# Hybrid SSD and GLA trunk on one core: z of two groups, and the values of a head pair, projected together with weights 512 columns wide

## The chip, the core and the metric

One core of a Trainium2 chip runs the whole layer in one launch. The time is device time in microseconds (us): the median of several executions. Beside it stands one execution that the hardware profiler recorded; its rows are what the text reads. TensorE (PE) multiplies, with its weight loads (PEld) beside it; VectorE (DVE), ScalarE (ACT) and GpSimd (POOL) do the rest; SyncE (SP) mainly starts transfers. L12 is line 12 of the kernel file.

## The reference, cut to what matters

The model width is 1024, the sequence 2048 tokens behind 16 meta tokens, one layer. One projection of the normalized input `u` gives everything; two branches run as recurrences (16 SSD heads in 4 groups; 4 GLA heads of 128 keys and 256 values); gates merge them.

```python
proj = jnp.einsum('bld,dn->bln', u, w_in)
z, xbc, dt_raw, q, k, v, g_gla, a_lr, merge_g = split_cols(proj, IN_WIDTHS)
xbc = jax.nn.silu(causal_depthwise_conv(xbc, conv_w, conv_b))
...
y_m, s_m = ssd_chunked(xs[:, :m], dt[:, :m], a, bm[:, :m], cm[:, :m], N_META, s0)
y_r, _ = ssd_chunked(xs[:, m:], dt[:, m:], a, bm[:, m:], cm[:, m:], SSD_CHUNK, s_m)
y = jnp.concatenate([y_m, y_r], axis=1) + d_skip[:, None] * xs
y = y.reshape(b, l, D_SSD) * jax.nn.silu(z)
y_ssd = rmsnorm(y.reshape(b, l, SSD_GROUPS, D_SSD // SSD_GROUPS),
                ssd_norm_w.reshape(SSD_GROUPS, -1)).reshape(b, l, D_SSD)
...
o_r, _ = gla_chunked(q[:, m:], k[:, m:], v[:, m:], log_a[:, m:], GLA_CHUNK, st_m)
o = rmsnorm(jnp.concatenate([o_m, o_r], axis=1), gla_norm_w)
y_gla = o.reshape(b, l, GLA_DV) * jax.nn.silu(g_gla)
branches = jnp.stack([y_ssd.astype(y_gla.dtype), y_gla], axis=2)
branch_proj = jnp.einsum('blnc,ncd->blnd', branches, w_branch)
gates = jax.nn.sigmoid(merge_g.reshape(b, l, N_BRANCH, D_MODEL))
merged = jnp.sum(gates * branch_proj, axis=2)
return hres + jnp.einsum('bld,de->ble', merged, w_out)
```

Each SSD group needs 256 columns of z, each GLA head 256 columns of v. Both are used with tokens on the partitions.

## The kernel before, in words

The kernel has two parts. The first goes through the sequence in four blocks of 512 tokens, computes the projections and both recurrences, and writes their outputs to DRAM. The second computes the gates, the branch products and the output product; the change leaves it as it is, but for two buffers that it reads at its start (below). Block 0 also carries the 16 meta tokens, so its feature-major projections run in two segments of 264 columns.

*Products.* An fp32 operand is split into two parts, high and low, each of TensorE's rounded fp32 type. `accum` makes one product out of three matmuls (high by high, high by low, low by high; L193 to L195 before, L203 to L205 after). K is 1024, in eight slices (`kt`) of 128.

*Weights.* `load_w` fetches 512 columns of weights into `whl` (four buffers, high and low). The first time, in block 0, it takes them raw, ScalarE and GpSimd split them, and the split pair is stored to DRAM; later blocks fetch that pair.

*Two kinds of projection.* Feature-major (`proj_feat`): the weights are TensorE's stationary operand and `u` streams, 512 columns at a time (`pj<-u,whl`). Token-major (`proj_tok`): 128 tokens of `u` are stationary and weights stream (`pj<-whl,u`). Before, z of one group and values of one head are 256 columns wide: four chunks of tokens, eight slices, three matmuls, 256 columns each, 96 matmuls. Two chunks share one PSUM bank (`halves_of`), so such a projection takes two banks. In block 0 the values of the meta tokens are one more chunk: the high and low meta rows side by side (`both`), two matmuls a slice (L227 before, L239 after), into a bank of `pt`. Group 0's z is projected with other columns, 288 wide, in a projection of its own (`zm`), into three banks of `pj` and one of `pt`.

*PSUM.* Eight banks: `pj` has three buffers (projections), `pt` three (transposes, sums), `pc` two (products of the scans).

*Order.* The program is written with generators. A projecting generator (`ssd_proj`, then `gla_proj`) yields after every step; a step of projection is 24 matmuls of 512 columns or, before, 48 of 256, about 5.5 us. At each yield `step()` advances every running scan (`ssd_scan`, `gla_scan`) and side job (`gates`, `fetch_u` for the next block's `u`, `beside_unit`) by one of its own yields. So a few scan instructions stand behind each projection step. TensorE's and SyncE's instructions stand in exactly this written order; those of VectorE, ScalarE and GpSimd are placed by the scheduler of the language, fixed at build time.

*One block.* Group 0 to 3: z (two steps; it yields once in the middle), then four feature tiles (x twice, B, C), each with a causal convolution (eviction at L528 and L529 on ScalarE, three VectorE steps, tanh and product). Then the group's scan begins (`begin(ssd_scan(...))`): per chunk of 128 tokens `before(c)` makes three transposes into a `pt` bank (L595 before, L626 after) and VectorE reads them three times (L598, L600, L601; after L629, L631, L632); `after(c)` makes `py` in a `pc` bank (L619 and L620; after L650, L651), `pst` in another (L623; after L654), and VectorE reads `py` twice (L628 and L631; after L659 and L662). At its end stand two turns (transposes, L655, after L686) into `pt` banks, which ScalarE reads (L657). Then head 0 to 3: query, key (`gla_keys`), values (two steps), two gates (`gla_gates`), and the head's scan. It starts with `kd` (L747), in block 0 copies the meta rows' `kd` (L803, after L866) and transposes them (L805, after L868); it builds the meta state (L819, after L882) and its copy (L820), levels of a masked product in `pc` banks (`level_out`, L789, after L852; merged by a predicated copy, L796), and ends with turns and their product (L916).

*Buffers in SBUF.* z, values and scan outputs use `tok4` (five buffers of 128x1024 fp32). `end_ot` and `end_g0`, `end_g1` hold the last head's output and gates until the second part.

Of the kernel before, what the change touches and what calls it, by code (L numbers as in the profile page):

```python
# [14 lines left out]
P = 128  # L15
# [5 lines left out]
SG = 4  # L21
# [19 lines left out]
def trunk_kernel(ctx: ExitStack, tc: tile.TileContext, xm, xmt, w_feat, w_tok, w_zm, w_br, w_o,  # L41
# [17 lines left out]
    end_ot = base.tile([P, NCH, 256], F32, name="end_ot")  # L59
    end_gs = [base.tile([P, BLK], F32, name=f"end_g{j}") for j in range(2)]  # L60
# [124 lines left out]

    def save(n):

        while len(unsaved) > n:
            nc.sync.dma_start(*unsaved.pop(0))
# [19 lines left out]
    def proj_tok(key, src, u, starts, banks, width=256, per=2, sub=None, both=None):  # L209

        nq = KT // per
        opened = set()
        for q0 in range(0, nq, 2):
            if q0 == nq // 2:
                yield
            ws = [load_w(f"{key}_{q}", src[:, q * per * width:(q + 1) * per * width]) for q in (q0, q0 + 1)]
            for i, ((bk, ps), a) in enumerate(zip(banks, starts)):
                c0 = sub if sub is not None and i >= NCH else 0  # L220
                for k2 in range(2 * per):
                    kt = q0 * per + k2
                    h, lo = ws[k2 // per]
                    cs = slice(k2 % per * width + c0, (k2 % per + 1) * width)
                    if both is not None and i >= NCH:
                        for part in (h, lo):
                            nc.tensor.matmul(ps[:2 * META], both[:, kt], part[:, cs], start=kt == 0 and part is h,  # L227
                                             stop=kt == KT - 1 and part is lo)
                        continue
                    accum(ps[:, c0:width], tuple(t[:, kt, a:a + P] for t in u),  # L230
                          (h[:, cs], lo[:, cs]), bk not in opened, kt == KT - 1, skip_group_check=True)
                    opened.add(bk)
# [271 lines left out]
    def ssd_proj(o, g):  # L504
        m0, tt = o.m0, o.tt
        feats = []
        zs = mk(wk, [P, NCH, 256], F32, "tok4", bufs=NT4)
        if g == 0:
            pss = [bank(*pl) for pl in [(pj, "pj")] * 3 + [(pt, "pt")] + ([(pc, "pc")] if m0 else [])]
            yield from proj_tok("zm", w_zm, o.u, o.starts + [0] * o.ci0, list(enumerate(pss)), 288, 1, 256)  # L510
            begin(dt_chain(o, pss[NCH:] + pss[:NCH]))
            done = [(ps[:, :256], zs[:, c]) for c, ps in enumerate(pss[:NCH])]
        else:
            pss, places = halves_of(pj, "pj")
            yield from proj_tok(f"z{g}", w_tok[g], o.u, o.starts, places)
            done = [(ps, zs[:, 2 * r:2 * r + 2].rearrange("p c f -> p (c f)")) for r, ps in enumerate(pss)]
        for ps, dst in done:
            nc.scalar.activation(dst, ps, AF.Tanh, scale=0.5)
            nc.vector.scalar_tensor_tensor(dst, dst, 1.0, ps, op0=ALU.add, op1=ALU.mult)
        yield  # L520
# [19 lines left out]
        begin(ssd_scan(o, g, feats, zs))  # L540
# [7 lines left out]
    def ssd_scan(o, g, feats, zs):  # L548
# [64 lines left out]
        def after(c):  # L613
# [19 lines left out]
            nc.vector.tensor_tensor(yt[:, c], yof, zs[:, c], op=ALU.mult)  # L633
# [37 lines left out]

    def gla_values(o, h):
# [9 lines left out]
        yield from proj_tok(f"v{h}", w_tok[SG + h], o.u, o.starts + [0] * o.ci0, places, both=o.both)  # L682
# [6 lines left out]
    def gla_gates(o, h, gs):  # L689
        t0 = T_GLA + 4 * h  # L690
        end = o.b == nblk - 1 and h == GH - 1
        for j in range(2):
# [6 lines left out]
            gg = end_gs[j] if end else mk(wk, [P, BLK], F32, "gg", bufs=4)  # L699
# [5 lines left out]
    def gla_proj(o, h):  # L705
        got = {"gs": []}
        keys = yield from gla_keys(o, h)
        last = o.b == nblk - 1
        if last and h == GH - 1:
            begin(gla_scan(o, h, *keys, got))  # L710
            yield
            got["v"] = yield from gla_values(o, h)
            yield
            yield from gla_gates(o, h - 1, held_gates.pop())
            yield from gla_gates(o, h, got["gs"])
        else:
            yield
            got["v"] = yield from gla_values(o, h)
            if last and h == GH - 2:
                begin(gla_scan(o, h, *keys, got))  # L720
                held_gates.append(got["gs"])
                yield
            else:
                yield
                yield from gla_gates(o, h, got["gs"])
                begin(gla_scan(o, h, *keys, got))

    held_gates = []

    def gla_scan(o, h, qs, kf, got):  # L730
# [145 lines left out]
        ot = end_ot if very_last else mk(wk, [P, NCH, 256], F32, "ot", bufs=1)  # L876
# [44 lines left out]
    def begin(gen):  # L921
        begun.append(gen)
# [13 lines left out]
    with tc.manual_schedule(engines={mybir.EngineType.PE, mybir.EngineType.SP}):  # L936
        for b in range(nblk):
            o = new_block(b, next_u[b])
            for i in range(SG + GH):
                if (b, i) in beside:  # L940
                    begin(beside_unit(beside[b, i]))
                if i == 1:
                    begin(gates(o))
# [251 lines left out]
    with tc.manual_schedule(engines={mybir.EngineType.PE, mybir.EngineType.SP}):  # L1195
        run(-1)
        for i, (st, n, p) in enumerate(order):
            step_no[0] = i
            st.product(n, p)
            if i == 1:  # L1200
                gla_turn(end_ot, end_gs, pb, "psb")
# [7 lines left out]
def _layout(inputs):  # L1209
# [26 lines left out]
    w_tok = tiles(np.concatenate([cols(o_z, 1024), cols(o_v, 1024)], axis=1), 256)  # L1236
# [34 lines left out]
    return {"xm": xm, "xmt": xmt, "w_feat": w_feat, "w_tok": w_tok, "w_zm": w_zm, "w_br": w_br, "w_o": w_o, "cf32": cf32, "cmsk": cmsk.reshape(P, -1),  # L1271
# [21 lines left out]
```

## Time and profile before

| what | value |
|---|---|
| time, median of 3 executions | 2274.29 us (2273.98 to 2274.93) |
| profiled execution: its time, its span | 2277.34 us, 2275.6 us |
| mean granted TensorE clock | 0.996 |
| TensorE busy | 2216.7 us, 12599 matmuls |
| VectorE, ScalarE, GpSimd busy | 1626.3, 1119.0, 511.8 us |
| moved by DMA | 507.50 MB, mean 223 GB/s |

The span runs from the first to the last recorded instruction; the time of an execution takes in what lies around it. Busy time is a sum over instructions; for TensorE the matmuls are pipelined and the recorded ends are modelled, so the time of a row of matmuls is best read as the distance between two places in the timeline. A wait is given as `engine buffer line <- engine that released it, its buffer and line: total us, how many, longest`. A row of the timeline is start, length, engine, line and operation, `out<-in`, the two tile shapes in partitions and columns, the number of them, and in brackets a wait ahead of it with its releaser. A row of a stretch is its bounds, its length, then busy time and count, the granted clock, the DMA share and GB/s.

### The profile page before, as it was taken

What the parts mean: (1) busy time and instruction counts of PE and PEld (TensorE: products, weight loads), DVE (VectorE), ACT (ScalarE), POOL (GpSimd) and SP (SyncE); (2) the same over time, 40 slices, a digit from 0 to 9 for tenths busy, and PEclk for the clock granted to TensorE, in tenths of its full rate; (3) what the DMA queues carried; (4) which work ended last, traced back from release to release, by engine and by line L of the source; (5) the groups of instructions that cost most, each with busy time, mean ns of one, the idle gap of its engine ahead of it and who ended that gap; (6) DMA issues with size and microseconds to landing.
All of it is one profiled execution on the core that took longest, in us unless ns stands there. A gap on an engine that the chain in (4) does not pass through costs nothing.

```text
span 2275.6 us, 36414 instructions
## 1 busy us (share of the span) xinstructions
PE 2216.7 (97%) x12599; PEld 1936.4 (85%) x12599; DVE 1626.3 (71%) x3332; ACT 1119.0 (49%) x2508; POOL 511.8 (22%) x645
## 2 busy tenths in 40 slices
PE   6899999999999999999999999989999999999997
PEld 6899888889888988888988898868888888888886
DVE  5787766687775578676569755786778866787866
ACT  5565654454444444443455443464644545554443
POOL 3344533122321222221122100012111112111212
PEclk9999999999999999999999999999999999999999
DMA  7666865667886676887577655465769866878753
GB/s 255 223 227 228 300 231 208 208 196 239 266 281 204 196 221 216 267 269 228 185 225 225 220 189 166 154 228 193 255 216 293 242 203 201 283 269 232 206 164 111
DMA packets 281865, 507.50 MB, mean 223 GB/s; under 512 B 27104, under 2 KB 134880, under 8 KB 281680
## 3 DMA queue, kind: packets, MB, share of 16 engines
q1 hardware_dynamic: 217232, 413.76, 55.9%
q0 software_dynamic: 17568, 50.87, 7.2%
q10 hardware_dynamic: 46880, 40.54, 5.4%
q8 instruction: 99, 1.62, 0.3%
q14 instruction: 86, 0.70, 0.1%
HBM read 357.87 MB, written 147.19 MB: 222 GB/s over the span
## 4 chain that ended last, share of the span: by engine, by line
PE 79%; DVE 8%; DMA 5%; issue 3%; ACT 3%; POOL 1%; SPq 1%; ACTq 0%; POOLq 0%; DVEq 0%
PE pj L193 13%; PE pj L195 12%; PE pj L194 12%; PE psa L193 6%; PE psa L194 6%; PE psa L195 6%; PE psb L194 3%; PE psb L193 3%; PE psb L195 3%; PE pc L619 2%; PE pc L789 2%; PE psc L194 1%; PE psc L193 1%; PE psc L195 1%; PE pc L620 1%
## 5 line engine op out<-in xcount | busy, mean ns | idle before, releaser
L193 PE MATMUL pj<-u,whl 128*128 128x512 f32 (+1 forms) x1184 | 445.8, 377 | 10.0 <-ACT acc L529 5.0
L195 PE MATMUL pj<-u,whl 128*128 128x512 f32 (+1 forms) x1184 | 430.1, 363 | 0.0
L194 PE MATMUL pj<-u,whl 128*128 128x512 f32 (+1 forms) x1184 | 429.3, 363 | 0.0
L193 PE MATMUL pj<-whl,u 128*128 128x256 f32 (+1 forms) x992 | 288.6, 291 | 2.3 <-ACT u L261 2.2
L195 PE MATMUL pj<-whl,u 128*128 128x256 f32 (+1 forms) x992 | 282.2, 284 | 0.2 <-DVE u L266 0.2
L194 PE MATMUL pj<-whl,u 128*128 128x256 f32 (+1 forms) x992 | 282.0, 284 | 0.0
L193 PEld LDWEIGHTS pj<-u,whl 128*128 128x128 f32 x1184 | 224.1, 189 | 47.7 <-ACT acc L529 6.1
L195 PEld LDWEIGHTS pj<-u,whl 128*128 128x128 f32 x1184 | 223.7, 189 | 35.6
L193 PE MATMUL psa<-b,a 128*128 128x512 f32 x640 | 249.8, 390 | 4.1 <-ACT sn L1063 4.1
L194 PEld LDWEIGHTS pj<-u,whl 128*128 128x128 f32 x1184 | 224.3, 189 | 33.0
L195 PE MATMUL psa<-b,a 128*128 128x512 f32 x640 | 249.3, 390 | 0.7 <-DVE a L1047 0.7
L194 PE MATMUL psa<-b,a 128*128 128x512 f32 x640 | 249.1, 389 | 0.0
L193 PEld LDWEIGHTS pj<-whl,u 128*128 128x128 f32 x992 | 189.7, 191 | 4.1 <-ACT u L261 2.3
L195 PEld LDWEIGHTS pj<-whl,u 128*128 128x128 f32 x992 | 189.5, 191 | 0.8 <-DVE u L266 0.8
L194 PEld LDWEIGHTS pj<-whl,u 128*128 128x128 f32 x992 | 189.8, 191 | 0.4
L181 POOL TENSOR_TENSOR whl<-wr,whl 128x512 fp32r<-128x512 f32 (+1 forms) x100 | 138.8, 1395 | 187.1 <-ACT whl L180 150.9
L533 DVE SCALAR_TENSOR_TENSOR acc<-cin,hcw,acc 128x512 f32<-128x512 f32 (+1 forms) x192 | 160.4, 835 | 13.1 <-ACT acc L529 10.9
L1047 DVE TENSOR_TENSOR a<-ar,a 128x512 fp32r<-128x512 f32 x160 | 109.9, 690 | 82.0 <-ACT a L1046 81.3
L84 POOL TENSOR_TENSOR wr<-wr 128x256 f32<-128x256 f32 x80 | 72.3, 904 | 423.0 <-DMA wr<-u 159.9
L1022 ACT ACTIVATE b<-br 128x512 fp32r<-128x512 f32 x196 | 118.3, 626 | 58.2 <-DMA br<-br_t 19.8
L193 PEld LDWEIGHTS psa<-b,a 128*128 128x128 f32 x640 | 120.2, 188 | 31.2 <-ACT sn L1063 6.2
L195 PEld LDWEIGHTS psa<-b,a 128*128 128x128 f32 x640 | 120.2, 188 | 26.4 <-DVE a L1047 1.4
(297 smaller groups left out, 4839.1 us busy)
## 6 DMA issues: line engine op xcount, KB each, us to landing
whl<-k_s SPq DMA_DIRECT2D x96, 512.0 KB, 4.5
whl<-k_g SPq DMA_DIRECT2D x96, 512.0 KB, 4.2
whl<-k_v SPq DMA_DIRECT2D x48, 512.0 KB, 4.0
whl<-k_z SPq DMA_DIRECT2D x36, 512.0 KB, 3.9
wr<-in_w_feat SPq DMA_DIRECT2D x64, 256.0 KB, 4.4
k_s<-whl SPq DMA_DIRECT2D x32, 512.0 KB, 3.8
cb<-cumd ACTq DMA_DIRECT2D x64, 256.0 KB, 5.7
k_g<-whl SPq DMA_DIRECT2D x32, 512.0 KB, 3.9
```

The source lines that it names most:

```text
L84: (nc.vector if store is None else nc.gpsimd).tensor_tensor(o, x, y, op=ALU.subtract)
L181: nc.gpsimd.tensor_tensor(hl[:, 1], raw, hl[:, 0].bitcast(F32), op=ALU.subtract)
L193: nc.tensor.matmul(ps, sh, mh, start=first, stop=False, **kw)
L194: nc.tensor.matmul(ps, sh, ml, start=False, stop=False, **kw)
L195: nc.tensor.matmul(ps, sl, mh, start=False, stop=last, **kw)
L533: nc.vector.scalar_tensor_tensor(acc, cin[:, k:k + tt], hcw[:, ti, k:k + 1], acc, op0=ALU.mult, op1=ALU.add)
L619: nc.tensor.matmul(py[:, h * 64:(h + 1) * 64], dm[:, h], xdt[:, h], start=True, stop=True)
L620: nc.tensor.matmul(py[:, 256:512], cf[:, a:a + P], s_ssd[:, g], start=True, stop=True)
L789: nc.tensor.matmul(ps[:, r * P:(r + 1) * P], kq[:, 2 * r * P:(2 * r + 1) * P], kq[:, (2 * r + 1) * P:(2 * r + 2) * P], start=True, stop=True)
L1022: nc.scalar.activation(t[:, 0], raw, AF.Copy)
L1047: nc.vector.tensor_tensor(t[:, 1], src, t[:, 0].bitcast(F32), op=ALU.subtract)
```

## The change

- Group 1's z and group 2's z are projected together (`z12`), with weights 512 columns wide, after group 1's feature tiles. Each of the four token chunks fills a whole bank: the three of `pj` and one of `pt` (`four_banks`). The projection takes four steps of 24 matmuls. Group 1's scan begins at its second yield, and z of group 1 is looked up when the scan multiplies by it; group 2 has no projection of z. Group 0 and group 3 project z as before.
- The values of heads 0 and 1, and of 2 and 3, are projected together (`gla_pair`), in the even head, 512 columns wide, in four steps and four banks. The odd head's values wait in SBUF: for head 1 in two tiles (`shared`) that hold the last head's output and gates later, for head 3 in `tok4`. In the even head the scan begins ahead of its gates; the odd head has keys, gates, scan.
- In block 0 the pair's meta rows, 512 columns, accumulate in a `pc` bank.
- In the last block heads 2 and 3 keep projections of 256 columns; their weights are the halves of the stored wide arrays, so each `whl` takes two transfers (`load_half`).
- Evictions of a wide bank (tanh and product for z, split in two parts for values) are made per 256 columns. The block's `gates` begin at group 3 instead of group 1.

```diff
+    def load_half(key, q, head):
+        hl = mk(wpool, [P, 2, 512], F32R, "whl", bufs=4)
+        for k in range(2):
+            nc.sync.dma_start(hl[:, :, k * 256:(k + 1) * 256].bitcast(F32),
+                              kept[f"{key}_{2 * q + k}"][:, :, head * 256:(head + 1) * 256])
+        return hl[:, 0], hl[:, 1]
...
-    def proj_tok(key, src, u, starts, banks, width=256, per=2, sub=None, both=None):
+    def proj_tok(key, src, u, starts, banks, width=256, per=2, sub=None, both=None, head=None):
         nq = KT // per
+        every = 2 if width == 512 else nq // 2
         for q0 in range(0, nq, 2):
-            if q0 == nq // 2:
+            if q0 and q0 % every == 0:
                 yield
...
     def ssd_proj(o, g):
-        else:
+        elif g == 3:
             pss, places = halves_of(pj, "pj")
...
-        begin(ssd_scan(o, g, feats, zs))
+        if g == 1:
+            pss = four_banks()
+            o.zs = {}
+            for i, _ in enumerate(proj_tok("z12", w_z12, o.u, o.starts, list(enumerate(pss)), 512, 1)):
+                if i == 1:
+                    begin(ssd_scan(o, g, feats, lambda: o.zs[1]))
+                yield
+            for gg in (1, 2):
+                o.zs[gg] = mk(wk, [P, NCH, 256], F32, "tok4", bufs=NT4)
+            silu([(ps[:, i * 256:(i + 1) * 256], o.zs[1 + i][:, c]) for c, ps in enumerate(pss) for i in range(2)])
+            yield
+        else:
+            begin(ssd_scan(o, g, feats, lambda: o.zs[2] if g == 2 else zs))
+
+    def four_banks():
+        return [bank(*pl) for pl in [(pj, "pj")] * 3 + [(pt, "pt")]]
...
+    def gla_pair(o, h):
+        pss = four_banks()
+        places = list(enumerate(pss))
+        if m0:
+            pv5 = bank(pc, "pc")
+            places.append((NCH, pv5))
+        yield from proj_tok(f"v{h // 2}", w_v[h // 2], o.u, o.starts + [0] * o.ci0, places, 512, 1, both=o.both)
+        vs = [(mk(wk, [P, NCH, 256], F32R, "tok4", bufs=NT4), mk(wk, [P, NCH, 256], F32R, "tok4", bufs=NT4)),
+              (shared(F32R), shared(F32R)) if h == 0 else
+              (mk(wk, [P, NCH, 256], F32R, "tok4", bufs=NT4), mk(wk, [P, NCH, 256], F32R, "tok4", bufs=NT4))]
+        if m0:
+            for i in range(2):
+                vms[i] = mk(wk, [P, 256], F32, "c1", bufs=NC1)[:2 * META]
+                nc.scalar.activation(vms[i], pv5[:2 * META, i * 256:(i + 1) * 256], AF.Copy)
+        for c, ps in enumerate(pss):
+            for i in range(2):
+                split(vs[i][0][:, c], vs[i][1][:, c], ps[:, i * 256:(i + 1) * 256])
...
     def gla_proj(o, h):
+        if not (last and h >= 2):
+            if h % 2 == 0:
+                yield
+                pair = yield from gla_pair(o, h)
+                (got["v"], pairs[h + 1]) = [(v, vm) for v, vm in pair]
+                yield
+                begin(gla_scan(o, h, *keys, got))
+                yield from gla_gates(o, h, got["gs"])
+            else:
+                yield
+                got["v"] = pairs.pop(h)
+                yield from gla_gates(o, h, got["gs"])
+                begin(gla_scan(o, h, *keys, got))
+            return
...
-                if i == 1:
+                if i == 3:
                     begin(gates(o))
```

Three places show how instructions stand before and after. A row is line, operation, `out<-in`, the shape and, behind an x, how many stand in a row. The number behind a name is only a running one.

TensorE in block 0, the end of the values of head 0 and the scan instructions behind it, before (L595 transposes of `before(c)`, L619 and L620 `py`, L623 `pst`):

```order
L227 MATMUL pt_3065<-whl_3168,both_378 32x256 x4
L227 MATMUL pt_3065<-whl_3175,both_378 32x256 x4
L595 MATMUL pt_3244<-cst,act_2507 128x128
L595 MATMUL pt_3244<-cst,act_2604 128x128
L595 MATMUL pt_3244<-cst,act_2719 128x128
L619 MATMUL pc_3262<-c_434_3034,sq_3041 128x64 x4
L620 MATMUL pc_3262<-s_ssd,act_2832 128x256
L623 MATMUL pc_3268<-c_435_3036,bt_3039 128x256
```

TensorE at the same place after, the values of the first pair:

```order
L239 MATMUL pc_2973<-whl_3139,both_375 32x512 x2
L239 MATMUL pc_2973<-whl_3146,both_375 32x512 x2
L626 MATMUL pt_3180<-cst,act_2389 128x128
L626 MATMUL pt_3180<-cst,act_2476 128x128
L626 MATMUL pt_3180<-cst,act_2597 128x128
L650 MATMUL pc_3198<-c_468_3095,sq_3102 128x64 x4
L651 MATMUL pc_3198<-s_ssd,act_2729 128x256
L654 MATMUL pc_3204<-c_469_3097,bt_3100 128x256
```

The meta rows' bank has moved from `pt` to `pc`, one of two; `py` and `pst`, which stand right behind one another, both need a `pc` bank as well. VectorE of after one step earlier, where the same chain reads `pt_3091` and `py` in `pc_3109`:

```order
L629 TENSOR_TENSOR c_468_3095<-pt_3091,tkd_367 128x256
L631 TENSOR_TENSOR c_469_3097<-pt_3091,wde_370 128x256
L632 TENSOR_TENSOR tok_430_2935<-pt_3091,pv 128x256
L842 TENSOR_TENSOR sq_3417<-sq_3416,act_2846 128x4x64
L844 TENSOR_TENSOR sq_3417<-sq_3416,act_2773 128x2x64 x2
L659 TENSOR_TENSOR c_474_3119<-pc_3109,ecu_371 128x256
L837 TENSOR_TENSOR sq_3494<-g_all_374 128x512
L662 TENSOR_TENSOR c_474_3119<-c_474_3119,pc_3109 128x256
```

Between the three reads of the transposes and the two reads of `py` (L659, L662) now stand L842, L844 and L837, which prepare levels of the head's scan (L779, L781 and L774 before).

VectorE in block 0, where the first GLA scan copies the meta rows' `kd` (L803), before; `acc` and `u` in L257 and L266 belong to the next block's `u`:

```order
L747 TENSOR_TENSOR act_3528<-act_3528,act_2937 128x528
L257 SCALAR_TENSOR_TENSOR acc_3759<-acc_3759,pv,cin_3458 128x512
L752 TENSOR_TENSOR act_3540<-act_3540,act_2870 128x512
L774 TENSOR_TENSOR sq_3784<-g_all_377 128x512
L631 TENSOR_TENSOR c_527_3515<-c_527_3515,pc_3505 128x256
L803 COPY bt_3633<-act_3528 128x32
L266 TENSOR_TENSOR u_2932<-acc_3759,u_2932 128x512
```

VectorE there after (the copy is L866, products of the next block's `u` are L269):

```order
L659 TENSOR_TENSOR c_514_3317<-pc_3307,ecu_371 128x256
L866 COPY bt_3480<-act_3400 128x32
L837 TENSOR_TENSOR sq_3584<-g_all_374 128x512
L662 TENSOR_TENSOR c_514_3317<-c_514_3317,pc_3307 128x256
L657 TENSOR_TENSOR s_ssd<-s_ssd,pc_3313 128x256
L269 SCALAR_TENSOR_TENSOR acc_3331<-acc_3331,pv,cin_3329 128x512
L269 SCALAR_TENSOR_TENSOR acc_3333<-acc_3333,pv,cin_3329 128x512
```

The copy has moved ahead of L837 (L774 before) and ahead of the products of the next `u`.

TensorE in block 1 where the z projection ends, before (end of `z2`; L655 are turns of a group's output, L579 the products of the next scan):

```order
L194 MATMUL pj_6784<-whl_6858,u_2932 128x256
L195 MATMUL pj_6784<-whl_6858,u_2932 128x256
L655 MATMUL pt_6916<-cst,tok_1034_6460 128x128 x4
L655 MATMUL pt_6924<-cst,tok_1034_6460 128x128 x4
L579 MATMUL pc_6932<-act_6762,act_6682 128x128 x4
L595 MATMUL pt_6943<-cst,act_6520 128x128
L595 MATMUL pt_6943<-cst,act_6598 128x128
L595 MATMUL pt_6943<-cst,act_6682 128x128
L193 MATMUL pj_6961<-u_2932,whl_6962 128x512
```

TensorE there after (end of `z12`):

```order
L204 MATMUL pt_5785<-whl_5978,u_2841 128x512
L205 MATMUL pt_5785<-whl_5978,u_2841 128x512
L686 MATMUL pt_6026<-cst,tok_942_5579 128x128 x4
L686 MATMUL pt_6034<-cst,tok_942_5579 128x128 x4
L626 MATMUL pt_6044<-cst,act_5462 128x128
L626 MATMUL pt_6044<-cst,act_5541 128x128
L626 MATMUL pt_6044<-cst,act_5639 128x128
L650 MATMUL pc_6062<-c_1020_5962,sq_5969 128x64 x4
L651 MATMUL pc_6062<-s_ssd,act_5724 128x256
L654 MATMUL pc_6068<-c_1021_5964,bt_5967 128x256
L203 MATMUL pj_6079<-u_2841,whl_6080 128x512
```

The last chunk of `z12` stands in a `pt` bank, and the two turns and the transposes behind it want three more of the three `pt` banks: the first two turns take the others, and the transposes the one that comes free next.

66 lines of the change are left out of this document (38 added, 28 removed).

## The prediction

> **What bounds the kernel now.** I read the page's busy shares and chain first, then the stretches, the waits of TensorE, and single steps.
>
> ```profile
> span 2275.6 us, 36414 instructions
> ...
> PE 2216.7 (97%) x12599; PEld 1936.4 (85%) x12599; DVE 1626.3 (71%) x3332; ACT 1119.0 (49%) x2508; POOL 511.8 (22%) x645
> ...
> PE 79%; DVE 8%; DMA 5%; issue 3%; ACT 3%; POOL 1%; SPq 1%; ACTq 0%; POOLq 0%; DVEq 0%
> ```
>
> TensorE bounds: 97% busy, 79% of the chain. Time it saves is time saved, wherever nothing else holds it. Two stretches (length; PE, PEld, DVE, ACT and POOL busy; clock; DMA) show where that is:
>
> ```profile
> 57.00:114.00 57.00, 50.64 (x376) 48.30 (x375) 41.12 (x76) 31.41 (x73) 20.06 (x21) 0.94 0.68 222
> 684.00:912.00 228.00, 226.99 (x1404) 202.49 (x1405) 157.63 (x359) 108.36 (x271) 48.49 (x67) 1.00 0.66 209
> ```
>
> From block 1 on TensorE idles about 1 us in 228, with VectorE at 69%. Early in block 0 it idles 6.4 us in 57. Its waits name the causes (total, times, longest):
>
> ```profile
> PE pj L193 <- ACT acc L529: 5.0, 4, 2.1
> PE pj L193 <- ACT g_all L491: 3.5, 2, 2.5
> PE pt L805 <- DVE bt L803: 2.5, 1, 2.5
> ```
>
> All of these lie in block 0. The sum is made against the profiled execution (2277.34 us, span 2275.6); the median of the runs is 2274.29, 3.05 less, and I take the same difference off it. A measurement here can tell about 0.2%, 4.5 us.
>
> **1. Wider matmuls.** Between two steps of the generators TensorE does a step of projection. Old token-major steps have 48 matmuls of 256 columns, feature-major ones 24 of 512. Here are two of each, taken after the same scan instructions, and last 24 uninterrupted matmuls of 512 in the second part (one more starts in the window):
>
> ```profile
> 699.90:705.73 5.83, 5.83 (x48) 1.00 0.45 169
> 743.07:748.91 5.84, 5.84 (x48) 1.00 0.45 163
> ...
> 707.42:712.99 5.57, 5.57 (x24) 1.00 0.88 294
> ...
> 750.59:756.13 5.54, 5.54 (x24) 1.00 0.78 270
> ```
>
> ```profile
> 1799.67:1805.11 5.44, 5.44 (x25) 1.00 0.83 202
> ```
>
> A changed step also becomes 24 matmuls of 512 columns. I take 5.835 - 5.555 = 0.28 us; the ends are 5.83 - 5.57 = 0.26 and 5.84 - 5.44 = 0.40. Changed steps: z of groups 1 and 2, four in each of four blocks, 16; values, two a head, 14 heads, 28 (the last block's heads 2 and 3 stay narrow). 44 x 0.28 = **12.3 us saved** (11.4 to 17.6), all on TensorE, some 9 us of it where TensorE never waits. The meta rows' matmuls halve in number and double in width: nothing. The number of steps between the starts of GLA scans stays six, so what the scans find around them hardly moves.
>
> The Trainium skill ("TensorE: Matmul & The Clock Gate", Back-to-back issue gap) gives N/2.4 + 2.5 ns from one warm matmul to the next, by which two halves cost only 2.5 ns more than one whole: 1056 merged pairs would save 2.6 us by that. The rows disagree: 5.835/48 is 121.6 ns and 5.555/24 is 231.5, so a pair saves 11.7 ns.
>
> **2. One accumulator bank in block 0.** The pair's meta rows accumulate in a `pc` bank, where a head's used `pt`. `pc` has two buffers, so for four projection steps one is left. The scan's `py` and `pst`, one behind the other on TensorE, must share it: `pst` waits until VectorE has read `py` twice. On VectorE these reads now stand behind six other instructions and around a seventh (L837). Old prices at this place (start, length) are:
>
> ```profile
> 246.74 0.49 PE L595 MATMUL pt<-cst,act 128*128 128x128 f32 x3
> ...
> 247.27 0.42 DVE L598 TENSOR_TENSOR c<-pt,tkd 128x256 f32<-128x256 f32 x1
> ...
> 248.28 0.52 DVE L779 TENSOR_TENSOR sq<-sq,act 128x256 f32<-128x256 f32 x1
> 248.40 0.59 PE L623 MATMUL pc<-c,bt 128*128 128x256 f32 x2
> ```
>
> ```profile
> 273.40 0.48 DVE L781 TENSOR_TENSOR sq<-sq,act 128x128 f32<-128x128 f32 x2
> 273.80 0.42 DVE L628 TENSOR_TENSOR c<-pc,ecu 128x256 f32<-128x256 f32 x1
> ...
> 279.65 0.68 DVE L774 TENSOR_TENSOR sq<-g_all 128x512 f32<-128x512 f32 x1
> 280.25 0.41 DVE L631 TENSOR_TENSOR c<-c,pc 128x256 f32<-128x256 f32 x1
> ...
> 280.58 0.17 DVE L803 COPY bt<-act 128x32 f32<-128x32 f32 x1
> ...
> 280.81 0.28 PE L805 MATMUL pt<-cst,bt 128*32 128x128 f32 x1 [2.47 <-DVE bt L803]
> ```
>
> L623 (`pst`) started 1.66 us after the transposes. VectorE reaches the end of its three reads of them at 1.54; then follow L842 (old L779) 0.44 to the next start, L844 twice 0.48, L659 (old L628) 0.42, L837 (old L774) 0.68, L662 (old L631) 0.41: 3.97, less some 0.1 of overlap, 3.9. So `pst` is 2.2 us late, twice in the first pair: 4.4. If only the two reads stood there it would be 0.8 each.
>
> In the second pair the GLA scan uses the bank for its state and its levels:
>
> ```profile
> 335.74 0.69 PE L819 MATMUL pc<-c,bt 32*128 32x256 f32 x2
> 336.36 1.30 PE L789 MATMUL pc<-sq 128*128 128x128 f32 x8
> 336.47 0.42 DVE L820 COPY s_gla<-pc 128x256 f32<-128x256 f32 x1 [5.10 <-PE pc L819]
> 337.18 0.45 DVE L796 COPY_PREDICATED c<-msk,pc 128x256 f32<-128x256 uint8 x1 [0.29 <-PE pc L789]
> ```
>
> The first level must now wait for the copy (336.89 instead of 336.36, with the way back 0.6), the second for the first one's predicated copy (0.45 and two hand-overs, 0.6): 1.2. One step later two levels come behind two turns of an output, whose VectorE products stand ahead of the predicated copy:
>
> ```profile
> 344.96 1.06 PE L789 MATMUL pc<-sq 128*128 128x128 f32 x8
> ...
> 346.09 1.40 DVE L916 SCALAR_TENSOR_TENSOR gg<-pt,hgw,gg 128x512 f32<-128x512 f32 x2
> ```
>
> The products 1.40 and the copy 0.45 from about 0.7 after the turns' start, against 1.3 for the second level: 1.3 late. **Together 6.9 us lost** (2 x 0.8 + 1.2 + 0.5 = 3.3 to, with 0.7 us of other VectorE work each time, 10).
>
> **3. The first GLA head's scan.** L805 waited 2.47 us for the copy L803, which stood on VectorE behind products of the next block's `u`. It now stands ahead of that group. I take all of it: **2.5 us back** (0 to 2.5).
>
> **4. Later banks and new neighbours.** Four banks, among them all three of `pj`, fill in a wide projection, and the next one needs the first. The first bank ends three quarters of a q-pair, about 4 us, before the last, and scan work stands between. Block 1's `zm` fills the same four banks, and the projection behind it took 24 matmuls in 5.65, as any other:
>
> ```profile
> 424.08:429.73 5.65, 5.64 (x24) 1.00 1.03 326
> ```
>
> So I charge nothing there; the cover is those 4 us, and without them two halves of a bank through ScalarE and VectorE would be exposed. But at z's end a third `pt` bank is now held, and before(1)'s transposes need the bank of the turn just made:
>
> ```profile
> 559.91 1.04 PE L655 MATMUL pt<-cst,tok 128*128 128x128 f32 x8
> ...
> 560.60 1.26 ACT L657 ACTIVATE gg<-pt,hsw 128x512 f32<-128x512 f32 x2
> 560.78 1.06 PE L579 MATMUL pc<-act,act 128*128 128x128 f32 x8
> ```
>
> The first copy ends at 561.23, while the transposes could start at 560.78: 0.5 us in blocks 1 to 3, 1.5. In block 0 two feature tiles now follow others with no scan work between; a wait on the bank's eviction (L529) averaged 1.25 there, a covered one nothing: 0.7 each, 1.4. The gates' start moves from group 1 to group 3 with the same two banks beside the same two steps; their 3.5 us in block 0 move along. Weight bytes are the same; the last block's narrow heads read them in half-width pieces through SP, some 16 more issues, whl four deep ahead. Evictions split in two cost ScalarE and VectorE fixed time, hidden at 49% and 71%. **2.9 us lost** (0 to 8).
>
> **Sum:** -12.3 + 6.9 - 2.5 + 2.9 = -5.0; 2274.3 - 5.0 = **2269.3 us**.
>
> **Rivals.** *Cheap bank:* VectorE is ahead and item 2 costs its low end with item 4 at half: -12.3 + 3.3 - 2.5 + 1.5 = -10.0, 2264. For it: VectorE was idle 5.10 us ahead of L820. Against: its order puts other work between.
>
> *Half clock:* a TensorE wait of this length was followed by a stretch at half clock:
>
> ```profile
> 63.28 0.39 PE L193 MATMUL pj<-u,whl 128*128 128x264 f32 x1 [2.06 <-ACT acc L529]
> ```
>
> ```profile
> 63.90:67.30 3.40, 3.40 (x18) 0.50 0.95 323
> ```
>
> That is 1.7 us more for each; the 2.47 us wait above had none. Two or three of the new waits would give 2273 to 2274, no change. The Trainium skill (same page, Part 1) has the clock fall after an idle window of about 3.4 us; by that these waits cost no clock, but here 2.06 us was enough.
>
> *Operand, not width:* the short rows also stream `u`, not weights. If the excess per pair belongs to that, width might save only 2.5 ns a pair, 2.6 us: 2274.3 - 2.6 + 6.9 - 2.5 + 2.9 = 2279. Against: the second part streams its `b` at 5.44.
>
> *Exposed evictions, slower:* at each of eleven wide ends TensorE waits for the first bank because eight half-bank evictions stand in ScalarE's and VectorE's queues out of its order. Eight at 0.42 are 3.4 us; with half of it exposed, 1.7 x 11 = 18.7, the time is 2288. It turns slower than 0.2% from 0.87 us an end. Against: `zm`'s row.
>
> **Numbers.** Forecast case 0.54, cheap bank 0.13, half clock 0.21, operand 0.03, exposed evictions 0.09. The forecast case spans 2265 to 2273; a little over half of it lies below 2269.7. Faster 0.54 x 0.6 + 0.13 = 0.46; slower 0.10; same 0.44. The range, 2261 to 2277, takes in cheap bank and half clock and leaves out most of the last two.
>
> **What would show it.** Right: for each of the three lines of the accumulation `pj<-whl,u` 128x512 x264, with x88 more under `pt` (the fourth bank), and 128x256 down from x896 to x192; a wide step of 24 matmuls in 5.5 to 5.6; waits of L654 on VectorE near 2.2, twice, in block 0's first pair, of L852 in its second; none of L868. Wrong: waits on `pj` for L571 or L259 in blocks 1 to 3, or a wide step over 5.7.

## The result, and the profile after

The changed kernel takes 2312.17 us (2307.70 to 2318.89, 5 executions); the kernel before, beside it, 2274.29 (2272.39 to 2274.93). The ratio is 1.0166, 95% interval 1.0154 to 1.0177: slower by 37.9 us. The page of the profiled execution (2314.49 us):

```profile
span 2312.7 us, 34352 instructions
PE 2227.7 (96%) x11511; PEld 1890.8 (82%) x11511; DVE 1625.9 (70%) x3376; ACT 1126.5 (49%) x2552; POOL 519.7 (22%) x645
PE 73%; DVE 13%; DMA 6%; ACT 3%; issue 3%; POOL 1%; SPq 1%; ACTq 0%; POOLq 0%; DVEq 0%
```

TensorE has 1088 matmuls fewer and is busy 11 us longer; on the chain its share fell by 6 points and VectorE's rose by 5. The next two tables cut both kernels at the start of each block's `zm` and at the start of the second part (stretch, length; busy time of PE, PEld, DVE, ACT, POOL; granted clock; DMA). Before:

```profile
22.00:405.60 383.60, 369.96 (x2650) 345.72 (x2651) 283.56 (x570) 213.55 (x524) 161.39 (x140) 0.99 0.71 240
405.60:762.90 357.30, 354.91 (x2167) 315.36 (x2165) 250.59 (x583) 164.44 (x407) 79.50 (x108) 1.00 0.71 229
762.90:1120.00 357.10, 354.48 (x2162) 314.99 (x2161) 250.87 (x582) 164.45 (x406) 80.00 (x108) 1.00 0.73 231
1120.00:1488.40 368.40, 364.79 (x2239) 324.25 (x2237) 250.26 (x602) 170.17 (x423) 50.88 (x69) 1.00 0.60 193
1488.40:2275.00 786.60, 767.67 (x3371) 631.62 (x3370) 582.75 (x981) 396.32 (x729) 135.56 (x211) 0.99 0.70 224
```

After:

```profile
22.00:429.10 407.10, 379.57 (x2330) 334.13 (x2331) 284.32 (x581) 214.87 (x535) 165.63 (x140) 0.97 0.67 226
429.10:790.90 361.80, 355.25 (x1879) 302.70 (x1877) 252.11 (x595) 167.15 (x419) 82.37 (x108) 0.99 0.70 226
790.90:1152.70 361.80, 353.43 (x1875) 301.38 (x1873) 250.34 (x594) 167.01 (x418) 82.13 (x108) 1.00 0.71 228
1152.70:1523.70 371.00, 365.25 (x2046) 315.32 (x2044) 248.38 (x609) 171.83 (x431) 49.72 (x69) 1.00 0.59 191
1523.70:2312.00 788.30, 769.32 (x3371) 632.83 (x3370) 582.27 (x981) 395.56 (x729) 135.43 (x211) 0.99 0.70 223
```

Block 0 lost 23.5 us, blocks 1 to 3 lost 4.5, 4.7 and 2.6, the second part 1.7. Length less busy time is TensorE's idle time, and one less the mean granted clock, times the span, is what half clock took. Idle time is counted from the first `zm` on. That gives a ledger, in us; most of the experiments below stand in it too.

| kernel | span | idle | clock, and its loss | rest |
|---|---|---|---|---|
| before | 2275.6 | 41.2 | 0.996, 9.1 | 2225.3 |
| after | 2312.7 | 67.2 | 0.988, 27.8 | 2217.7 |
| before, gates at group 3 | 2282.7 | 41.1 | 0.994, 13.7 | 2227.9 |
| before, meta rows in `pc` | 2280.1 | 41.2 | 0.994, 13.7 | 2225.2 |
| only z wide | 2295.3 | 51.2 | 0.992, 18.4 | 2225.7 |
| only values wide | 2292.0 | 50.3 | 0.990, 22.9 | 2218.8 |
| after, meta rows in `pt` | 2305.1 | 64.0 | 0.990, 23.1 | 2218.0 |
| after, products halved | 2318.0 | 64.2 | 0.990, 23.2 | 2230.6 |
| values wide from block 1 on | 2267.2 | 39.4 | 0.996, 9.1 | 2218.7 |

The rest is work at full clock, with the same start ahead of the first `zm` in every row, good to about 1.2 us since the clock has three digits. Going from before to after, work fell by 7.6, waits rose by 26.0 and clock loss by 18.7: 37.1, the difference of the spans. Where TensorE waited inside a stretch at half clock, the ledger counts that time as idle and half of it as clock loss too. Counted by TensorE's busy time inside these stretches alone, the loss is 4.9 before and 22.1 after: 17.2 more, and work fell by 6.2. The waits of TensorE after (total, times, longest):

```profile
PE pc L654 <- DVE c L662: 7.0, 2, 3.5
PE pc L650 <- DVE sq L641: 5.3, 4, 1.5
PE pc L954 <- DVE s_gla L957: 5.3, 9, 1.9
PE pt L686 <- ACT tok L681: 5.3, 4, 2.1
...
PE pj L203 <- DVE tok L571: 3.4, 1, 3.4
PE pc L852 <- DVE s_gla L883: 3.3, 3, 1.8
...
PE pc L852 <- DVE c L859: 1.8, 3, 1.0
PE pt L626 <- ACT gg L688: 1.0, 3, 0.3
```

The wait for the copy of the meta rows' `kd` (2.5 before) is gone. The others are new or have grown, and most end with VectorE. Behind the three longest of those shown, TensorE then ran at half clock. These are stretches of 3.41 us around the end of the wide z in block 0 and the two waits of L654:

```profile
128.72:132.13 3.41, 0.67 (x3) 0.27 (x2) 3.38 (x8) 3.41 (x9) 1.65 (x2) 1.00 0.50 151
132.13:135.55 3.42, 2.77 (x12) 2.80 (x13) 2.51 (x7) 0.50 (x2) 1.30 (x1) 0.50 0.95 314
135.55:138.96 3.41, 3.41 (x17) 3.41 (x17) 0.00 (x0) 0.52 (x1) 0.00 (x0) 0.50 0.50 187
255.01:258.42 3.41, 1.84 (x14) 1.41 (x12) 2.86 (x6) 1.34 (x3) 2.76 (x3) 1.00 1.05 408
258.42:261.84 3.42, 1.47 (x4) 1.22 (x5) 2.82 (x7) 1.23 (x4) 0.39 (x1) 0.50 1.00 361
261.84:265.25 3.41, 3.41 (x10) 2.63 (x9) 0.25 (x1) 0.00 (x0) 0.00 (x0) 0.50 0.48 189
272.08:275.49 3.41, 0.55 (x3) 0.52 (x4) 3.34 (x7) 0.72 (x2) 1.31 (x2) 1.00 0.93 270
275.49:278.90 3.41, 3.41 (x10) 2.63 (x9) 0.93 (x3) 0.89 (x3) 0.00 (x0) 0.50 0.70 269
```

In the whole trace eleven stretches of half clock stand against four before. All begin on one raster of 3.413 us, and all but the last, at the kernel's end, are one or two such cells long. The five executions after go along with the clock too: 0.991 goes with 2307.70 and 2308.65 us, 0.988 with 2314.49 and 2318.89.

### The profile page after: what moved, and what is told of

Read it like the earlier page. It is cut to its first block, busy times and chain, and to the rows that moved or that the text cites. A ratio compares the mean times of both kernels' runs of the same rounds, so it can differ in the third digit from the quotient of the medians.

```text
span 2312.7 us, 34352 instructions
## 1 busy us (share of the span) xinstructions
PE 2227.7 (96%) x11511; PEld 1890.8 (82%) x11511; DVE 1625.9 (70%) x3376; ACT 1126.5 (49%) x2552; POOL 519.7 (22%) x645
## 4 chain that ended last, share of the span: by engine, by line
PE 73%; DVE 13%; DMA 6%; ACT 3%; issue 3%; POOL 1%; SPq 1%; ACTq 0%; POOLq 0%; DVEq 0%
PE pj L203 11%; PE pj L205 11%; PE pj L204 11%; PE psa L203 5%; PE psa L204 5%; PE psa L205 5%; PE psb L203 3%; PE psb L204 3%; PE psb L205 3%; PE pc L852 2%; PE pc L650 2%; DMA cb<-cumd 1%; PE psc L204 1%; PE psc L203 1%; PE psc L205 1%
## 5 line engine op out<-in xcount | busy, mean ns | idle before, releaser
L203 PEld LDWEIGHTS pj<-u,whl 128*128 128x128 f32 x1184 | 226.5, 191 | 48.6 <-ACT acc L540 5.6
L205 PEld LDWEIGHTS pj<-u,whl 128*128 128x128 f32 x1184 | 226.1, 191 | 35.6
L204 PEld LDWEIGHTS pj<-u,whl 128*128 128x128 f32 x1184 | 226.9, 192 | 32.9
L203 PE MATMUL pj<-whl,u 128*128 128x512 f32 (+2 forms) x552 | 197.1, 357 | 3.6 <-ACT u L273 2.2
L204 PE MATMUL pj<-whl,u 128*128 128x512 f32 (+2 forms) x552 | 188.4, 341 | 0.6 <-POOL whl L184 0.6
L205 PE MATMUL pj<-whl,u 128*128 128x512 f32 (+2 forms) x552 | 188.1, 341 | 0.2 <-DVE u L278 0.2
L203 PEld LDWEIGHTS psa<-b,a 128*128 128x128 f32 x640 | 120.1, 188 | 30.3 <-ACT sn L1128 5.3
L205 PEld LDWEIGHTS psa<-b,a 128*128 128x128 f32 x640 | 120.1, 188 | 26.5 <-DVE a L1112 1.5
L204 PEld LDWEIGHTS psa<-b,a 128*128 128x128 f32 x640 | 120.1, 188 | 24.6
L1111 ACT ACTIVATE a<-ar 128x512 fp32r<-128x512 f32 x160 | 99.2, 625 | 66.5 <-PE psb L205 50.5
L1088 DVE TENSOR_TENSOR b<-br,b 128x512 fp32r<-128x512 f32 x196 | 128.3, 685 | 3.9 <-ACT b L1087 3.9
```

Of the source, the lines that this page charges most:

```text
L203: nc.tensor.matmul(ps, sh, mh, start=first, stop=False, **kw)
L204: nc.tensor.matmul(ps, sh, ml, start=False, stop=False, **kw)
L205: nc.tensor.matmul(ps, sl, mh, start=False, stop=last, **kw)
L1088: nc.vector.tensor_tensor(t[:, 1], raw, t[:, 0].bitcast(F32), op=ALU.subtract)
L1111: nc.scalar.activation(t[:, 0], src, AF.Copy)
```

## The experiments

**Gates late, alone.** In the kernel before, `gates` begin at group 3.

```diff
-                if i == 1:
+                if i == 3:
                     begin(gates(o))
```

> The kernel before, with one line changed: the block's gates begin at group 3 instead of group 1, as in the changed kernel. Theory (late gates): in the changed kernel, waits of TensorE on VectorE and ScalarE work of the scans (L650 <- L641, L686 <- L681, L650 <- L657) total 12.3 us in blocks 1 to 3 against 2.7 before, and the trace shows the gates' work (L502 to L511) among it; with about 7 us of half clock behind those waits, gates alone should bring 2274 to 2283-2290. Rival (the wide z's eviction delays that work, gates are harmless by themselves): 2273-2277.

Measured: 2284.49 us against 2276.03, ratio 1.0040 (1.0027 to 1.0052), 8.5 slower, inside the theory's range. Blocks 1 to 3 are 9.1 us longer, but only 3.0 of that is idle time, and block 0 and the second part lost 1.1 and 2.0 of it, so idle time did not grow in sum. The clock loss grew by 4.6 and the work by 2.6; where this work comes from isn't shown. The turns of a group now wait more often:

```profile
PE pt L655 <- ACT tok L650: 5.2, 5, 1.6
```

It was 1.6 in two waits. In the changed kernel the same place in block 1 reads, on VectorE, ScalarE and TensorE:

```profile
621.52 1.36 DVE L511 TENSOR_TENSOR_SCAN g_all<-ones_r,tok 128x128 f32<-128x128 f32 x4
...
627.15 0.42 DVE L664 TENSOR_TENSOR tok<-c,tok 128x256 f32<-128x256 f32 x1
...
627.80 0.58 ACT L696 ACTIVATE act<-pj 128x512 f32<-128x512 f32 x1
628.28 0.41 ACT L666 ACTIVATE junk<-tok 128x256 bf16<-128x256 f32 x1
...
630.11 1.71 ACT L681 ACTIVATE tok<-tok,rstd 128x256 f32<-128x256 f32 x4 [1.33 <-POOL rstd L254]
630.67 1.28 PE L686 MATMUL pt<-cst,tok 128*128 128x128 f32 x3 [2.14 <-ACT tok L681]
```

The gates' running sums (L511) and the next block's `u` now share VectorE and ScalarE with the end of group 2's scan, so its last product (L664) and its sum of squares (L666) come late. How much of the wait of 2.14 us is theirs was not measured.

**Gates one group earlier in the changed kernel.**

```diff
-                if i == 3:
+                if i == 2:
                     begin(gates(o))
```

> The changed kernel, gates begun at group 2 instead of group 3. Late gates: the waits behind group 2's scan in blocks 1 to 3 fall back towards 3 us and take their half-clock stretches along, so 2312 falls to 2298-2304. Rival (the eviction of the wide z): no change, 2306-2314, since those evictions stand where they stood.

Measured: 2330.31 us, ratio 1.0242 (1.0226 to 1.0258), slower still. Both expectations missed. The gates need banks of `pj` and `pt` right behind the wide z, which has filled all three of `pj`, and the waits for banks and for the scans' results grow:

```profile
PE pt L686 <- ACT tok L681: 9.8, 4, 3.5
PE pc L650 <- DVE sq L641: 7.8, 5, 3.1
PE pj L500 <- ACT g_all L503: 7.1, 4, 2.4
```

So the late start can't be taken back by one group in this order. A start at group 1, as in the kernel before, was not run with the wide z.

**Only z wide**, with gates at group 3, and values as before:

```diff
+        yield from proj_tok(f"v{h}", w_v[h], o.u, o.starts + [0] * o.ci0, places, both=o.both)
...
-        if not (last and h >= 2):
-            if h % 2 == 0:
```

> Only z of groups 1 and 2 is projected 512 wide, with gates at group 3; values of each head as before. Adding the terms that the trace of the changed kernel shows: late gates +14, the wait behind the wide z's end in block 0 (3.4) and the half clock behind it (3.4), 16 wide steps at -0.18: about 2274 + 18 = 2292. If the order of the value pairs makes the waits in blocks 1 to 3, 2274-2280 instead.

Measured: 2298.42 against 2276.01, ratio 1.0098 (1.0085 to 1.0111), 22.4 slower, where 18 had been added up. Less what late gates cost alone, 8.5, the wide z costs 13.9.

**Only values wide**, z and gates as before:

```diff
-        if g == 1:
-            pss = four_banks()
...
+        begin(ssd_scan(o, g, feats, lambda: zs))
...
-                if i == 3:
+                if i == 1:
                     begin(gates(o))
```

> Only the value pairs are projected 512 wide, z of each group and the gates' start at group 1 as before. Terms: the single pc bank in block 0 +11 and the half clock behind it +5, 28 wide steps at -0.18 = -5: 2285. If the pc bank costs only waits, and half clock comes from elsewhere: 2280. If the loss belongs to z and gates alone: 2268-2272.

Measured: 2290.60, ratio 1.0059 (1.0044 to 1.0073), 14.6 slower, where 11 had been added up. The two halves add up: 22.4 + 14.6 = 37.0 against 37.9.

**The meta rows' bank.** The pair's meta rows accumulate in `pt` in the changed kernel:

```diff
-            pv5 = bank(pc, "pc")
+            pv5 = bank(pt, "pt")
             places.append((NCH, pv5))
```

> The changed kernel, with the pair's meta rows in block 0 in a pt bank, so that the scans have both pc banks again. Theory (the single pc bank): the two waits of L654 on L662 (7.0 us) and those of L852 (3.9) go, and two stretches of half clock behind them (6.83 and 3.41 us long, worth 5.1): 2312 falls by 11 to 16, to 2296-2301. Rival (pt, with one buffer left for the transposes in those steps, becomes the wait): 2308-2316, with waits of L626 on L632 instead.

Measured: 2302.39, ratio 1.0113 (1.0097 to 1.0128), 9.8 less than after by the medians and 12 by the ratios; 11 to 16 were expected. The waits of L654 are gone, block 0 is 9.2 us shorter (397.9 against 407.1), 6.7 of it idle time. Of the 3.9 that the levels (L852) waited for their state's copy and for one another in block 0, 1.8 stayed, so that part does not belong to the bank.

The same line in the kernel before, the other way round:

```diff
-            pv5 = bank(pt, "pt")
+            pv5 = bank(pc, "pc")
             places.append((2, pv5[:, :256]))
```

> The kernel before, with the bank of each head's meta rows in block 0 moved from pt to pc, one line; matmul widths and order as before. The prediction's price for the single pc bank was 6.9 us of waits: 2276 becomes 2283. With the longer waits that the changed kernel showed (3.5 instead of 2.2 for each pst, 3.9 for levels) and half clock behind them, 10 to 16: 2286-2292. If the wait belongs to the pair's order and not to the bank: 2274-2278.

Measured: 2281.83 against 2275.64, ratio 1.0025 (1.0014 to 1.0036), 6.2 slower, close to the 6.9, but not by the mechanism behind that number. `pst` (L623) never waits for VectorE in this trace. The levels do: L789 waits 3.7 us in block 0, where the kernel before has no such wait, and block 0 is 5.6 us longer, 2.5 of it idle time. Three stretches of half clock stand in block 0 against two, and two of the three (at 84 and 146 us) lie ahead of the first meta rows; idle time in sum did not grow, and two of the seven executions (2276.48 and 2277.03) were hardly slower than the kernel before. So the bank by itself costs the levels some waits. The long waits of `pst` came only with the changed order, in which L842, L844 and L837 stand in front of the reads.

**Width by itself.** The changed kernel in its own order, each product of 512 columns as two of 256:

```diff
+                    for w0, w1 in ((0, 256), (256, 512)) if width == 512 else ((c0, width),):
+                        ws_ = slice(k2 % per * width + w0, k2 % per * width + w1)
+                        accum(ps[:, w0:w1], tuple(t[:, kt, a:a + P] for t in u), (h[:, ws_], lo[:, ws_]),
+                              bk not in opened, kt == KT - 1, skip_group_check=True)
+                        opened.add(bk)
```

> The changed kernel in its own order, but each product of 512 columns made as two of 256, so that width alone is undone. By the trace of the changed kernel a wide step takes 5.66 us and a narrow one took 5.84, 44 steps: 2312 rises by 7.9, to 2320. By the prediction's price (0.28 a step) it rises by 12.3, to 2324. If width saves nothing at all (operand, not width): 2310-2314.

Measured: 2316.96, ratio 1.0182 (1.0169 to 1.0196), 4.8 above after, less than either price. The ledger tells why: work rose by 12.9, as the prediction's 12.3, while idle and clock loss happened to be 7.6 smaller. So width was priced rightly, and total times that differ by a few stretches of half clock do not show it by themselves.

**The clock by itself.** A kernel of projection steps, with a few transposes between them; `gap(k, ...)` is a chain of k + 1 VectorE operations between two matmuls:

```diff
+        for k in (1, 3, 5, 7, 9, 11, 13, 15):
+            for i in range(14):
+                gap(k, step(512))
+                step(512)
+                step(512)
```

> Leaves the whole computation out. TensorE makes steps of 24 products of 512 columns, with one gap every three steps: it waits for a chain of VectorE operations whose length grows in eight stages from about 0.7 to about 3.5 us, 14 gaps each, so that a gap falls at all places of the 3.41 us raster on which the half-clock stretches of both traces start. Theory (raster): half clock follows where one raster window has more than about 1.4 to 1.9 us of idle TensorE, so gaps under 1.4 never bring it, gaps of 2.0 to 2.8 bring it where they lie in one window and not where a raster line splits them, and gaps over 3.4 nearly always. Rival (length): a gap above a fixed length always brings it, wherever it lies. Ahead of the gaps stand 5 steps each of 48 by 256 and 24 by 512 columns behind transposes, with and without an fp32 product as the scans make it: by the trace a wide step takes 5.56 behind transposes and 5.66 behind the fp32 product, a narrow one 5.84 behind either.

Measured, first the steps with equal neighbours: 48 by 256 and 24 by 512 columns, behind transposes, and then both behind transposes and an fp32 product (a matmul whose operands are not split, as `py` and `pst` are made):

```profile
61.90:67.73 5.83, 5.83 (x51) 5.83 (x50) 0.00 (x0) 0.00 (x0) 0.00 (x0) 1.00 0.01 3
118.23:123.80 5.57, 5.57 (x28) 4.55 (x27) 0.00 (x0) 0.00 (x0) 0.00 (x0) 1.00 0.00 0
93.49:99.43 5.94, 5.94 (x51) 5.91 (x49) 0.00 (x0) 0.00 (x0) 0.00 (x0) 1.00 0.01 3
148.03:153.70 5.67, 5.67 (x27) 4.62 (x26) 0.00 (x0) 0.00 (x0) 0.00 (x0) 1.00 0.00 0
```

Width saves 0.26 and 0.27 a step; the fp32 product ahead adds 0.1 to either, where the expectation had it for the wide step alone. Then two gaps of the same length, 3.31 us, as cells of the raster:

```profile
1361.45:1364.86 3.41, 1.60 (x8) 0.98 (x6) 1.60 (x6) 0.00 (x0) 0.00 (x0) 1.00 0.00 0
1364.86:1368.27 3.41, 1.91 (x9) 1.60 (x10) 1.31 (x5) 0.00 (x0) 0.00 (x0) 1.00 0.00 0
1368.27:1371.69 3.42, 3.42 (x17) 2.84 (x16) 0.00 (x0) 0.00 (x0) 0.00 (x0) 1.00 0.00 0
...
1381.93:1385.34 3.41, 1.12 (x5) 0.58 (x4) 2.04 (x7) 0.00 (x0) 0.00 (x0) 1.00 0.00 0
1385.34:1388.75 3.41, 2.39 (x6) 1.93 (x7) 0.87 (x3) 0.00 (x0) 0.00 (x0) 0.50 0.01 2
1388.75:1392.17 3.42, 3.42 (x9) 2.64 (x8) 0.00 (x0) 0.00 (x0) 0.00 (x0) 0.50 0.00 0
```

The first is split 1.81 and 1.50 by a raster line, and the clock stays. The second has 2.29 in one cell, and the two cells behind it run at half. Over all 112 gaps the split is clean: the 32 that leave at most 1.92 us idle in each cell are followed by no half clock, the 80 that leave 1.95 or more in one are all followed by it. The limit is a little above the 1.4 to 1.9 of the theory. Where the first cell at half clock was itself idle for 0.86 us or more, the next was at half too (44 times); with 0.69 or less it was not (36 times). The rival, a fixed length, fails on the first gap above: gaps of 2.01 us brought half clock where they lay in one cell.

**Waits filled.** In the changed kernel TensorE does 36 products of 128 columns that nobody reads, at the two waits of L654 and at the wide z's end in block 0:

```diff
+    def keep_warm(o, dst):
+        for _ in range(36):
+            nc.tensor.matmul(dst, o.u[0][:, 0, 0:P], o.u[0][:, 0, 0:P], start=True, stop=True, skip_group_check=True)
...
+                if warm["on"]:
+                    keep_warm(o, warm["ps"][:, 3 * P:])
                 pst = bank(pc, "pc")
```

> The changed kernel, with 36 products of 128 columns that nobody reads put into three of its waits in block 0: between py and pst in the two steps where pst waits 3.5 us for the pc bank, and behind the wide z's end, where the next projection waits 3.4. The waits stay, only TensorE works in them. Theory (idle TensorE in one raster window halves the next): the stretches at 132, 258 and 275 us (6.83, 6.83 and 3.41 long) vanish, worth 7.2 us: 2312 falls to 2305. Rival (half clock follows the late data or the DMA, not the idling): 2310-2315 with the stretches still there.

Measured: 2305.97, ratio 1.0140 (1.0120 to 1.0160), 6.2 less than after where 7.2 was expected; the intervals touch, so the trace has to carry it. None of the three places is at half clock any more:

```profile
128.72:132.13 3.41, 3.41 (x33) 3.41 (x33) 3.41 (x9) 2.66 (x8) 2.76 (x2) 1.00 0.59 187
132.13:135.55 3.42, 3.42 (x30) 3.42 (x30) 1.76 (x5) 0.36 (x2) 0.22 (x1) 1.00 0.97 322
...
255.01:258.42 3.41, 3.41 (x27) 3.27 (x27) 2.24 (x6) 1.24 (x4) 0.00 (x0) 1.00 0.99 344
258.42:261.84 3.42, 3.42 (x16) 2.78 (x16) 0.04 (x1) 0.00 (x0) 0.00 (x0) 1.00 0.33 129
```

The data come as late after `py` as they did: from the start of the two slow operations (L844 after) to the end of the last read of `py` (L662 after) VectorE takes 3.2 us in both kernels. The raster lies elsewhere in this execution, but that is not why: without the unread products one cell at each of the three places would be idle for 2.96, 3.27 and 2.69 us. Idling alone had made the clock fall.

**Values wide where nothing is tight.** Pairs in blocks 1 to 3, block 0, z and gates as before:

```diff
+    def load_pair(h2, q):
...
+                              kept[f"v{2 * h2 + k}_{q // 2}"][:, :, q % 2 * 256:(q % 2 + 1) * 256])
...
-        if not (last and h >= 2):
+        if o.b and not (last and h >= 2):
```

> Values of head pairs 512 wide in blocks 1 to 3 only (their weights put together from the stored narrow ones, two transfers each); block 0, z and the gates' start at group 1 as before. 20 wide steps (8, 8 and 4) at -0.28 us, the difference that stages of equal neighbours gave (5.84 against 5.56), are -5.6: 2270. If the pair order brings the waits and half clock that the run with only value pairs had in blocks 1 to 3 (they came to +3 in all there, by the lengths of the blocks): 2279. If the single pc bank of block 0 was the whole loss of that run: 2270 or less.

Measured: 2269.10 (2267.35 to 2271.16) against 2275.64, ratio 0.9972 (0.9962 to 0.9981): 6.5 faster, the only version that beats the kernel before. Work fell by 6.6, idle time by 1.8, and the clock stayed: in this kernel the pair order costs nothing measurable in blocks 1 to 3. The same pairs in the run with only values wide made these blocks 3.1 us longer than before, with stretches of half clock in them. Why they stayed away here was not separated from chance.

## Why the prediction was wrong

**The bound.** TensorE does bound, and saved work is saved time "wherever nothing else holds it". But more came to hold it than was listed, and each wait was added up at its own length, without the half clock behind it.

**Item 1, width: right.** 12.3 forecast, 12.9 by the halved products. The traces have the forecast number of wide products, and a step of 5.56 or, behind an fp32 product, 5.67. The order gave 5.3 of the 12.9 back as work (halved products against before). 0.1 for each step that now stands behind an fp32 product is a part of that, and the late gates alone came with 2.6; the rest is not accounted for. The 2.6 us of saving that the prediction quoted and set aside do not fit the 12.9, and "operand, not width" falls with them.

**Item 2, the single `pc` bank: right mechanism for `pst`, two thirds of the size.** 2.2 was forecast for each wait of L654, 3.5 came. The rows show the missing 1.3:

```profile
257.00 1.96 DVE L844 TENSOR_TENSOR sq<-sq,act 128x128 f32<-128x128 f32 x2
...
257.51 1.30 POOL L184 TENSOR_TENSOR whl<-wr,whl 128x512 fp32r<-128x512 f32 x1
...
260.37 1.19 PE L654 MATMUL pc<-c,bt 128*128 128x256 f32 x2 [3.52 <-DVE c L662]
```

Two operations that were priced at 0.48 took 1.96 while GpSimd split weights. The levels in the second pair waited 3.9 instead of 2.5. Together 10.9 for 6.9, before the clock; with both `pc` banks back, 1.8 of the levels' 3.9 stayed, so the bank's own share is nearer 9.

**Item 3, the first GLA scan: right.** The wait of 2.5 is gone.

**Item 4, banks and neighbours: wrong in what it left at nothing.** The `pt` bank at z's end cost 1.0 (1.5 forecast), and the feature boundaries in block 0 nothing (1.4). But "so I charge nothing there" failed at the wide z's end in block 0: the next projection waited 3.4 us for a bank. There the scan's VectorE work stood among the evictions:

```profile
130.81 1.49 DVE L641 TENSOR_TENSOR sq<-sq,sq 128x512 f32<-128x512 f32 x1
...
132.22 0.41 DVE L571 SCALAR_TENSOR_TENSOR tok<-tok,pj 128x256 f32<-128x256 f32 x1
...
132.78 0.56 PE L203 MATMUL pj<-u,whl 128*128 128x264 f32 x1 [3.38 <-DVE tok L571]
```

The quoted `zm` row was from block 1, where more stands between. At the z's end in block 0 TensorE had two matmuls (0.7 us) to do before it needed the bank. This is the rival of exposed evictions, at one end of eleven. And the gates' start "with the same two banks beside the same two steps" was looked at for its banks only; its VectorE and ScalarE work moved beside the next block's `u`, which costs 8.5 by itself. In blocks 1 to 3 idle time rose by 12 us (8.6 to 20.7) where about 1.5 was forecast. Item 1's "what the scans find around them hardly moves" failed too: TensorE's waits for the GLA state (L954 for L957, L889 for L892 before) grew from 2.1 to 5.3. Of the waits named as a sign of being wrong, on `pj` for L571 or L259 in blocks 1 to 3, none came; most of the loss lay in other waits.

**Half clock: left out of the sum.** It stood as a rival with a chance of 0.21 and "two or three of the new waits" at 1.7 us each. It was 18.7 us, half of the loss (17.2 by TensorE's busy time alone). The prediction had set 2.06 us with half clock behind it beside 2.47 without and took the matter as undecided. In raster cells the two agree: the 2.06 lay in one cell, the 2.47 was cut by a line. The rule cited from the Trainium skill (TensorE: Matmul & The Clock Gate, Part 1) has the window run free, 3413 ns long, and the rasters agree; its idle window, read as a window that is idle as a whole, does not agree, since 1.95 of 3.41 us sufficed.

Put together, -5.0 was forecast: -12.3 of width and 7.3 of waits. Measured: -7.6 of work, 26.0 of waits, 18.7 of clock. So two steps failed alike. The waits came 18.7 us above their price: 10.5 in blocks 1 to 3 and 3.4 at the wide z's end in block 0, where item 4 put the neighbours' VectorE and ScalarE work at nothing, and 4.0 in item 2. Half clock, which the sum had at nothing, added as much again.

## What to carry to other kernels

A TensorE that is 97% busy does not make narrow matmuls the first thing to widen: four banks instead of two, and work pushed beside other work, cost more here than 44 wide steps gave. Only the value pairs in blocks 1 to 3, with z, gates and block 0 as before, gained. Price a new wait twice: at its length, and, from about 2 us of idle time in one raster cell on, with half of the 3.4 us behind it, times the chance that it falls into one cell. When moving a side job, follow its VectorE and ScalarE instructions, not its banks alone, and don't take a cover from another block's row.

## What the runs showed of the hardware that was not expected

- The clock of TensorE follows idle time by raster cells of 3.413 us: 1.92 us or less in each cell never halved the next, 1.95 or more always did (112 gaps). In the traces of the whole kernel the limit is not that sharp: cells with 1.43 us idle (at 1221 us in the changed kernel) and with 1.05 (at 452 us with halved products) were followed by half clock, and one with 1.87 (at 279 us before) was not. What counts as activity there stays open.
- VectorE operations with two SBUF inputs (L781 before, L844 after) take 0.28 us, but 0.5 to 0.8 or 1.4 at times: 20 of 192 before and 27 of 192 after took over 0.4, and every one of them overlapped a GpSimd instruction; of those that overlapped none, none did. The Trainium skill (GPSIMD Engine Reference, Key points) has the two engines share SBUF interfaces; that fits, though no run here took the GpSimd work away.
- A step of matmuls takes 0.1 us longer behind transposes and a plain fp32 product than behind transposes alone, at both widths (5.94 against 5.84, 5.67 against 5.56).
